# Second block's experts: a fixed order on the tensor engine, and the first overflow block as a seventeenth expert

## The chip, the cores and the metric

The kernel runs on one core of a Trainium2 chip. The core has a tensor engine (PE, with its weight loads shown apart as PEld), a vector engine (DVE), a scalar engine (ACT), GpSimd (POOL) and a sync engine (SP) that here issues the weight transfers. Each engine has its own instruction stream and waits for the others on semaphores. The metric is the device time of one execution in microseconds. Before the change it was 1744.35 us, the median of 3 runs (1742.81 to 1746.68).

## The reference, cut to what matters

Two transformer trunks run one after the other on 256 tokens of width 1024, in float32. The change touches only the last stage: the mixture of experts of the second trunk. Each token picks 2 of 16 experts; an expert is a gated network with weights `w1`, `w3` (1024 x 512) and `w2` (512 x 1024). A final norm follows.

```python
def moe(x, router_w, router_b, w1, w3, w2):
    ...
    gates = jnp.sum(jax.nn.one_hot(eidx, N_EXPERTS, dtype=F32_2) * w[..., None], axis=1).astype(x.dtype)
    out = jnp.zeros_like(x)
    for e in range(N_EXPERTS):
        h = jax.nn.silu(x @ w1[e]) * (x @ w3[e])
        out = out + gates[:, e:e + 1] * (h @ w2[e])
    return out
...
        y = moe(hl2.reshape(B * S, D), router_w, router_b, lp['moe_w1'], lp['moe_w3'], lp['moe_w2'])
        xl = xl + g2_l * y.reshape(B, S, D)
...
    return rmsnorm(xl, final_g)
```

## The kernel before, in words

All weights of the program come through one ring of seven buffers of 2 MB (`RING = 7`), filled by transfers that SP issues in one fixed order (`Stream`, L317). A buffer is given to the next transfer when its last reader is done. In the last stage each expert has three such transfers, `w1`, `w3` and `w2`, so 48 for the 16 experts.

Experts are not run on all 256 tokens. After the router, `rank` holds each token's place in the list of its expert, and a block of 64 places per expert is computed. Where an expert has more than 64 tokens, the rest forms overflow blocks of 64 more places; up to seven such blocks are listed (`ji` holds their experts, `n_jobs` their number), and they are run after the sixteen experts in nested branches on `n_jobs` (L1872 to L1877).

Two experts with even and odd number form a pair and share their tiles:

- `take` (L1764) builds a one-hot matrix `oh` of the places on DVE, multiplies the normed tokens `n` by it (16 matmuls, L1777, with the two experts' 64 places side by side), and scales and shifts the result into `xg` in turns on DVE and ACT (L1784, L1781). Then it builds a second one-hot matrix `ohg` that holds the gates (L1788), transposes it on PE (L1792) and copies it to `sT` on ACT.
- `mlp` (L1796) is a generator with four steps per expert. Step 1: 16 matmuls with `w1` (L1807) and silu on ACT (L1814, `sg`). Step 2: 16 matmuls with `w3` and the product `hid` on DVE (L1818). Step 3: two transposes of `hid` on PE (L1822) and a copy to `hidT` on ACT (L1824). Step 4: 8 matmuls with `w2` (L1832) and the multiplication with the trunk's gate row into `Y` on DVE (L1837).
- `scatter` (L1751) multiplies `sT` with the `Y` of both experts (4 matmuls, L1755), and adds the result to `x` on DVE (L1756).

A matmul on float32 stands as two instructions in the profile and as one in the built program.

The loop (L1909 to L1920) writes the steps of expert e and expert e-1 alternately, and adds the scatter of an earlier pair and the `take` of the next one after odd experts. The order in which PE runs them is not the written one: the framework's scheduler sorts the instructions of each engine by its own estimate of when each is ready.

An overflow block (`job`, L1847) reads its expert number into an SP register, issues three transfers, selects its places (L1863 to L1867), and does `take`, the four steps and `scatter` with nothing else between. After it come the sums of squares on ACT, the products with the final norm's row on DVE and POOL (L1928), the root, and the output.

Of the kernel before, what the change touches and what calls it, by code (L numbers as in the profile page):

```python
# [19 lines left out]
D = 1024  # L20
S = 256
# [335 lines left out]
def trunk_kernel(ctx: ExitStack, tc: tile.TileContext, I: dict, O: dict):  # L357
# [1321 lines left out]
    def moe2(ss):  # L1679
        shsc = ada[2, 1]  # L1680
        with tc.tile_pool(name="moe2", bufs=1, reuse_waits="tile") as wk:
# [76 lines left out]
            def tiles(t="", nb=2):  # L1758
                k = dict(bufs=nb)
                return dict(oh=wk.tile([128, 2, 128], F32, name="oh" + t, **k), og=wk.tile([128, 2, 128], F32, name="ohg" + t, **k),  # L1760
                            xg=wk.tile([128, 8, 128], F32, name="xg" + t, **k), sT=wk.tile([128, S], F32, name="sT" + t, **k),
                            Y=wk.tile([128, D], F32, name="Y" + t, **k))

            def take(cols_, t, w=64):  # L1764

                m = w * len(cols_)
                oh, og, xg, sT = t["oh"], t["og"], t["xg"], t["sT"]
# [4 lines left out]
                for d4 in range(2):  # L1772
                    p = bank()
                    for j in range(4):
                        dt = 4 * d4 + j
                        for b in range(2):
                            T.matmul(p[:, j * 128:j * 128 + m], n[:, b, dt * 128:(dt + 1) * 128], oh[:, b, :m], start=b == 0, stop=b == 1)  # L1777
                    for j in range(4):
# [4 lines left out]
                        else:  # L1783
                            V.tensor_scalar(xg[:, dt, :m], p[:, j * 128:j * 128 + m], shsc[:, 1, dt:dt + 1],  # L1784
                                            shsc[:, 0, dt:dt + 1], op0=OP.mult, op1=OP.add)
                for b in range(2):
                    for i, (sl, gt) in enumerate(cols_):
                        v = V.tensor_scalar(og[:, b, w * i:w * i + w], it, sl[:, b:b + 1], gt[:, b:b + 1],  # L1788
                                            op0=OP.is_equal, op1=OP.mult)
                p = bank()  # L1790
                for b in range(2):
                    T.transpose(p[:m, b * 128:(b + 1) * 128], og[:, b, :m], ident)  # L1792
                A.copy(sT[:m], p[:m, :256])
                return v

            def mlp(e, xg, i, Y, get=None):  # L1796

                c = slice(64 * i, 64 * i + 64)
# [3 lines left out]
                def up(nm):  # L1802
                    w = weights(nm)
                    p = bank("u", 3)
                    for kt in range(8):
                        for h in range(2):
                            T.matmul(p[rows[h], :256], xg[:, kt, c], w[kt // 4][:, kt % 4, h * 256:(h + 1) * 256], start=kt == 0, stop=kt == 7)  # L1807
                    if get is None:
                        free((nm, e), 2)
                    return p  # L1810

                pg = up("w1")
# [3 lines left out]
                pu = up("w3")  # L1816
                hid = wk.tile([128, 256], F32, name="hid", bufs=2)
                V.tensor_tensor(hid, pu[:, :256], sg, op=OP.mult)  # L1818
                yield
# [208 lines left out]
```

## Time and profile before

| what | value |
| --- | --- |
| median of 3 runs | 1744.35 us (1742.81 to 1746.68) |
| profiled execution, own time | 1742.27 us |
| its span, first to last instruction | 1740.5 us |
| PE busy / PEld busy | 1313.8 us (75%) / 723.0 us (42%) |
| DVE busy / ACT busy / POOL busy | 487.8 us (28%) / 249.4 us (14%) / 10.7 us (1%) |
| data moved | 636.01 MB, mean 365 GB/s |
| mean granted clock of PE | 0.896 |

All rows below are of the profiled execution, whose own time is 1742.27 us: 1740.5 us of span and 1.77 us around it. The last stage begins at about 1432 us with the second trunk's second norm and runs to the end. Durations are of one instruction or of a merged run of equal instructions. A run of matmuls is shown with the time to the end of the last; the next run can start before that, so what a group costs PE is read from one start to the next. Bracketed numbers are idle time of the engine just ahead of the row, and what ended it.

### The profile page before, as it was taken

The numbers are of one execution on the slowest core, as the hardware profiler recorded it, in microseconds if no ns is written. First come the engines' busy times: TensorE is split into PE (matmuls) and PEld (weight loads), VectorE is DVE, ScalarE is ACT, GpSimd is POOL, SyncE is SP. The second block draws the span as 40 slices with busy tenths as digits, with TensorE's granted clock in tenths as the row PEclk, the third lists the DMA queues.
The fourth block names the chain that finished last, engine by engine and source line by source line (L and its number), as shares of the span: only waits on it lengthen the run. The fifth ranks groups of instructions, "written<-read, shape, count | busy, mean of one in ns | idle before, by whom it ended". The sixth has DMA issues, their size and how long they took to land. (4 is left out here: it accounts for less than half of the span.)

```text
span 1740.5 us, 24033 instructions
## 1 busy us (share of the span) xinstructions
PE 1313.8 (75%) x10612; PEld 723.0 (42%) x10612; DVE 487.8 (28%) x1051; ACT 249.4 (14%) x567; POOL 10.7 (1%) x19
## 2 busy tenths in 40 slices
PE   5997757756565569988575665657799998999996
PEld 2444423323222234545232232224487656555453
DVE  2444212402010029441111020100245726233223
ACT  3021100100000022511100000000223422111012
POOL 0000000000000000000000000000000000000000
PEclk9998988978888879998888787889999998999998
DMA  9978899999999998469999999999942765999970
GB/s 378 413 314 365 363 428 428 427 427 427 428 427 428 427 415 340 160 271 427 428 427 427 427 427 427 428 427 428 427 158 90 297 249 221 427 427 427 421 310 26
DMA packets 46972, 636.01 MB, mean 365 GB/s; under 512 B 6192, under 2 KB 6320, under 8 KB 8464
## 3 DMA queue, kind: packets, MB, share of 16 engines
q1 hardware_dynamic: 44624, 630.82, 86.6%
q0 software_dynamic: 1952, 3.09, 0.6%
q8 instruction: 85, 1.39, 0.3%
q10 hardware_dynamic: 288, 0.52, 0.1%
q14 instruction: 23, 0.19, 0.0%
HBM read 633.42 MB, written 1.05 MB: 365 GB/s over the span
## 5 line engine op out<-in xcount | busy, mean ns | idle before, releaser
L1065 PE MATMUL b<-w,xg 128*32 128x256 f32 x4096 | 316.6, 465 | 219.4 <-DMA w<-in_moe_w_up_dram 134.6
L1065 PEld LDWEIGHTS b<-w,xg 128*32 128x32 f32 x4096 | 148.9, 129 | 385.0 <-issue 137.7
L1065 PE MATMUL b<-w,hidT 128*32 128x256 f32 x2048 | 160.7, 467 | 83.2 <-DMA w<-in_moe_w_down_dram 77.7
L1085 DVE TENSOR_TENSOR hid<-b,sg 128x256 f32<-128x256 f32 x32 | 13.6, 425 | 504.0 <-PE b L1065 410.9
L1065 PEld LDWEIGHTS b<-w,hidT 128*32 128x32 f32 x2048 | 76.4, 129 | 154.5 <-DMA w<-in_moe_w_down_dram 62.3
L1807 PE MATMUL u<-w,xg 128*64 128x256 f32 x1088 | 125.0, 384 | 0.0
L1093 DVE SCALAR_TENSOR_TENSOR Y<-b,cc,gq 32x256 f32<-32x256 f32 x128 | 61.5, 480 | 211.7 <-PE b L1065 210.1
L499 DVE SCALAR_TENSOR_TENSOR w<-w,cond 128x1024 f32<-128x1024 f32 x77 | 97.0, 1280 | 4.9 <-DMA w<-in_ada21s_dram 3.2
L1807 PEld LDWEIGHTS u<-w,xg 128*64 128x64 f32 x1088 | 78.3, 138 | 47.5 <-issue 11.7
L1080 ACT ACTIVATE sg<-b 128x256 f32<-128x256 f32 x32 | 12.3, 383 | 416.4 <-PE b L1065 416.3
L1832 PE MATMUL b<-w,hidT 128*64 128x512 f32 x272 | 63.2, 598 | 9.8 <-ACT hidT L1824 9.8
L1090 ACT COPY hidT<-b 128x256 f32<-128x256 f32 x32 | 11.9, 372 | 320.6 <-PE b L1088 320.6
L707 PE MATMUL b<-w,n 128*128 128x512 f32 x128 | 56.0, 594 | 0.0
L1837 DVE TENSOR_TENSOR Y<-b,hkb 64x512 f32<-64x512 f32 x34 | 23.4, 688 | 72.2 <-PE b L1832 71.9
L1191 PE MATMUL b<-w,hT 128*128 128x512 f32 x96 | 43.4, 608 | 0.0
L832 PE MATMUL b<-w,hT 128*128 128x512 f32 x96 | 41.6, 593 | 1.7 <-DMA w<-in_fc_dram 1.7
L1777 PE MATMUL b<-oh,n 128*128 128x128 f32 (+1 forms) x288 | 39.3, 297 | 3.2 <-DVE oh L1771 3.2
L1777 PEld LDWEIGHTS b<-oh,n 128*128 128x128 f32 x288 | 36.8, 209 | 9.2 <-issue 6.3
L1106 PE MATMUL b<-Y,gT 128*128 128x512 f32 x64 | 32.6, 646 | 9.7 <-DVE Y L1093 9.7
L1000 PE MATMUL b<-oh,n 128*128 128x128 f32 x256 | 35.6, 305 | 0.9 <-DVE oh L1045 0.9
L1832 PEld LDWEIGHTS b<-w,hidT 128*64 128x64 f32 x272 | 18.6, 136 | 42.2 <-issue 28.3
L707 PEld LDWEIGHTS b<-w,n 128*128 128x128 f32 x128 | 24.0, 190 | 28.8 <-issue 28.7
(444 smaller groups left out, 1345.2 us busy)
## 6 DMA issues: line engine op xcount, KB each, us to landing
w<-in_moe_w_gate_dram SPq DMA_DIRECT2D x64, 2048.0 KB, 30.8
w<-in_moe_w_up_dram SPq DMA_DIRECT2D x64, 2048.0 KB, 30.9
w<-in_moe_w_down_dram SPq DMA_DIRECT2D x64, 2048.0 KB, 30.9
w<-in_moe_w_dram SPq DMA_DIRECT2D x51, 2048.0 KB, 14.9
w<-in_wi_dram SPq DMA_DIRECT2D x5, 2048.0 KB, 22.4
w<-in_ada00s_dram SPq DMA_DIRECT2D x4, 2048.0 KB, 22.6
w<-in_ada01s_dram SPq DMA_DIRECT2D x4, 2048.0 KB, 25.5
w<-in_ada10s_dram SPq DMA_DIRECT2D x4, 2048.0 KB, 11.5
```

Of the source, the lines that this page charges most:

```text
L499: V.scalar_tensor_tensor(into[:, hs], w[:, hs], c, into[:, hs], op0=OP.mult, op1=OP.add)
L707: T.matmul(acc, mixT[:, kt, b * 128:(b + 1) * 128], w(kt)[:, h * 512:(h + 1) * 512], start=kt == first, stop=kt == last)
L832: T.matmul(p, hT[:, kt, b * 128:(b + 1) * 128], w(kt), start=kt == 0, stop=kt == 7)
L1000: T.matmul(p[:, j * 128:(j + 1) * 128], n[:, b, dt * 128:(dt + 1) * 128], oh[:, b, g * 128:(g + 1) * 128], start=b == 0, stop=b == 1)
L1065: T.matmul(p[32 * q:32 * q + 32, :256], lhs(kt), w[:, k, q * 256:(q + 1) * 256], start=kt == 0, stop=kt == 7)
L1093: V.scalar_tensor_tensor(Y[32 * j:32 * j + 32, q * 256:(q + 1) * 256], pd[32 * q:32 * q + 32, :256], cc[32 * q:32 * q + 32, e:e + 1], gq[3 ...
L1106: T.matmul(p, gT[:, b * 128:(b + 1) * 128], Y[:, h * 512:(h + 1) * 512], start=True, stop=True)
L1191: T.matmul(p, hT[:, kt, b * 128:(b + 1) * 128], w(kt), start=kt == 0, stop=kt == 7)
L1777: T.matmul(p[:, j * 128:j * 128 + m], n[:, b, dt * 128:(dt + 1) * 128], oh[:, b, :m], start=b == 0, stop=b == 1)
L1807: T.matmul(p[rows[h], :256], xg[:, kt, c], w[kt // 4][:, kt % 4, h * 256:(h + 1) * 256], start=kt == 0, stop=kt == 7)
L1832: T.matmul(pd[rows[h]], hidT[:, kt % 2, rows[kt // 2]], w[kt // 2][:, kt % 2, h * 512:(h + 1) * 512], start=kt == 0, stop=kt == 3)
L1837: V.tensor_tensor(Y[c, h * 512:(h + 1) * 512], pd[rows[h]], gq2[rows[h]], op=OP.mult)
```

## The change: what it does

1. `take` is cut into `take` (gathering) and `way_back` (gates, transposes, copy to `sT`), and each step of `mlp`, as well as `take`, `scatter` and `way_back`, returns its last PE instruction. `turn_of` runs a step with every PE instruction ordered behind the last one of the step before (`tc.issue_after`). So PE runs the loop in the written order, and the scheduler has no choice there. The order on the other engines is not tied.
2. In the loop the `take` of the next pair, the scatter of the earlier pair and `way_back` now come after the even expert of a pair instead of the odd one.
3. The first overflow block is no longer inside a branch: its places are selected ahead of the loop (`job_slots(0)`), its weights are requested when expert 14 is written, and it runs as expert number 16 in the loop, with tiles of its own for `sT` and `Y` (`sTz`, `Yz`), whether or not an overflow exists.
4. Its scatter comes last, after the branches for the other six possible blocks.

```diff
             def scatter(sT, Y, k):
...
-                        T.matmul(p, sT[:k, b * 128:(b + 1) * 128], Y[:k, h * 512:(h + 1) * 512], start=True, stop=True)
+                        last = T.matmul(p, sT[:k, b * 128:(b + 1) * 128], Y[:k, h * 512:(h + 1) * 512], start=True, stop=True)
...
+                return last
...
+            tail = []
+
+            @contextmanager
+            def in_turn():
+                with ExitStack() as held:
+                    if tail:
+                        held.enter_context(tc.issue_after(tail[-1].ins))
+                    yield
...
-            def mlp(e, xg, i, Y, get=None):
+            def mlp(e, t, i, get=None):
...
-                if e in (E - 1, None):
+                if e is None:
                     table_of_roots(hidT[0:1, 0, 0:1])
-                yield
+                yield last
...
-            def jobs(j=0):
+            def jobs(j=1):
...
+            def turn_of(f):
+                with in_turn():
+                    last = f()
+                if last is not None:
+                    tail.append(last)
...
+            first_job = job_slots(0)
             for e in range(E + 1):
-                cur = mlp(e, ts[e // 2]["xg"], e % 2, ts[e // 2]["Y"]) if e < E else iter(())
-                next(cur, 0)
-                next(prev, 0)
-                next(cur, 0)
-                next(prev, 0)
-                if e % 2 == 1 and e >= 3:
-                    t = ts.pop((e - 3) // 2)
-                    scatter(t["sT"], t["Y"], 128)
-                if e % 2 == 1 and e + 1 < E:
-                    ts[(e + 1) // 2] = pair(e + 1)
+                cur = mlp(e, ts[e // 2], e % 2) if e < E else mlp(None, ts[E // 2], 0, first_ws)
+                for g in (cur, prev, cur, prev):
+                    turn_of(lambda: next(g, None))
+                if e % 2 == 0 and e < E:
+                    t2 = ts[e // 2 + 1] = dict(own="" if e + 2 < E else "z")
+                    cs = both_of(e + 2) if e + 2 < E else first_job
+                    turn_of(lambda: take(cs, t2))
+                    if e:
+                        t = ts.pop(e // 2 - 1)
+                        turn_of(lambda: scatter(t["sT"], t["Y"], 128))
+                    turn_of(lambda: way_back(cs, t2))
+                    if e + 2 == E:
+                        first_ws = job_weights(0)
                 prev = cur
+            turn_of(lambda: next(prev))
             t = ts.pop(E // 2 - 1)
-            scatter(t["sT"], t["Y"], 128)
+            turn_of(lambda: scatter(t["sT"], t["Y"], 128))
+            turn_of(lambda: next(prev))
             jobs()
+            t = ts.pop(E // 2)
+            scatter(t["sT"], t["Y"], 64)
```

How the instructions stand on PE. First one pair in the middle of the loop, before the change, from one scatter to the next. L1755 is the scatter, L1807 the matmuls with `w1` or `w3`, L1777 the `take`, L1792 the transposes to `sT`, L1822 those of `hid`, L1832 the matmuls with `w2`:

```order
L1755 MATMUL b<-Y,sT 128x512 x4
L1807 MATMUL u<-w,xg 64x256 x16
L1777 MATMUL b<-oh,n 128x128 x9
L1807 MATMUL u<-w,xg 64x256 x16
L1777 MATMUL b<-oh,n 128x128 x7
L1792 MATMUL b<-cst,ohg 128x128 x2
L1822 MATMUL b<-cst,hid 128x128 x2
L1832 MATMUL b<-w,hidT 64x512 x8
L1807 MATMUL u<-w,xg 64x256 x32
L1822 MATMUL b<-cst,hid 128x128 x2
L1832 MATMUL b<-w,hidT 64x512 x8
```

The same pair after the change, on PE (L1765 is the scatter now, L1825 the matmuls with `w1` or `w3`, L1787 the `take`, L1810 and L1840 the transposes, L1850 those with `w2`):

```order
L1787 MATMUL b<-oh,n 128x128 x16
L1765 MATMUL b<-Y,sT 128x512 x4
L1810 MATMUL b<-cst,ohg 128x128 x2
L1825 MATMUL u<-w,xg 64x256 x16
L1840 MATMUL b<-cst,hid 128x128 x2
L1825 MATMUL u<-w,xg 64x256 x16
L1850 MATMUL b<-w,hidT 64x512 x8
L1825 MATMUL u<-w,xg 64x256 x16
L1840 MATMUL b<-cst,hid 128x128 x2
L1825 MATMUL u<-w,xg 64x256 x16
L1850 MATMUL b<-w,hidT 64x512 x8
```

The same matmuls stand there. Before, the two transposes of `hid` stood directly in front of the matmuls with `w2` of the same expert; now 16 matmuls with the next expert's `w3` stand between them, and the `take` is in one piece.

The end of the loop on PE before, from the last expert to the overflow block's `take` (L1777 with 64 columns) and on to its scatter:

```order
L1807 MATMUL u<-w,xg 64x256 x32
L1822 MATMUL b<-cst,hid 128x128 x2
L1832 MATMUL b<-w,hidT 64x512 x8
L1755 MATMUL b<-Y,sT 128x512 x4
L1906 TENSOR_LOAD jobi
L1875 COMPARE_AND_BRANCH
L1777 MATMUL b<-oh,n 128x64 x16
L1792 MATMUL b<-cst,ohg 64x128 x2
L1807 MATMUL u<-w,xg 64x256 x32
L1822 MATMUL b<-cst,hid 128x128 x2
L1832 MATMUL b<-w,hidT 64x512 x8
L1755 MATMUL b<-Y,sT 128x512 x4
```

And now on PE, from the overflow block's `w1` (its `take` stands further up, among expert 14 and 15) to the branch:

```order
L1825 MATMUL u<-w,xg 64x256 x16
L1840 MATMUL b<-cst,hid 128x128 x2
L1825 MATMUL u<-w,xg 64x256 x16
L1850 MATMUL b<-w,hidT 64x512 x8
L1840 MATMUL b<-cst,hid 128x128 x2
L1765 MATMUL b<-Y,sT 128x512 x4
L1850 MATMUL b<-w,hidT 64x512 x8
L1935 TENSOR_LOAD jobi
L1904 COMPARE_AND_BRANCH
```

The overflow block's steps moved in between those of expert 15, and the scatter of the last pair moved ahead of the block's `w2`. PE's last rows now, after the six branch bodies, are these:

```order
L1825 MATMUL u<-w,xg 64x256 x32
L1840 MATMUL b<-cst,hid 128x128 x2
L1850 MATMUL b<-w,hidT 64x512 x8
L1765 MATMUL b<-Y,sT 128x512 x4
L1904 UNCONDITIONAL_BRANCH x7
L1765 MATMUL b<-Yz,sTz 128x512 x4
```

The last row is new there: before, PE had no matmul behind the branches.

## Rows read from the trace of the kernel before

**Rows 1.** Stretches: us, busy (count) of PE, PEld, DVE, ACT, POOL; clock, DMA share, GB/s
```profile
1520.00:1560.00 40.00, 38.03 (x242) 20.02 (x240) 13.40 (x28) 3.50 (x9) 0.00 (x0) 1.00 1.01 427
1703.00:1714.00 11.00, 8.93 (x51) 7.30 (x52) 3.75 (x15) 2.94 (x6) 0.00 (x0) 0.69 0.01 1
```

**Rows 2.** Waits of PE from 1447 us to the end: total us, times, longest
```profile
PE b L1832 <- ACT hidT L1824: 9.8, 15, 0.9
PE b L1822 <- DVE hid L1818: 4.7, 8, 0.6
```

**Rows 3.** Timeline of PE, one pair: start, us, engine, line, operation, count, idle before
```profile
1542.98 7.08 PE L1807 MATMUL u<-w,xg 128*64 128x256 f32 x64
1550.64 0.44 PE L1822 MATMUL b<-cst,hid 128*128 128x128 f32 x2 [0.58 <-DVE hid L1818]
1551.59 3.65 PE L1832 MATMUL b<-w,hidT 128*64 128x512 f32 x16 [0.52 <-ACT hidT L1824]
1555.18 3.70 PE L1755 MATMUL b<-Y,sT 128*128 128x512 f32 x8
1558.81 3.67 PE L1807 MATMUL u<-w,xg 128*64 128x256 f32 x32
...
1571.35 3.65 PE L1832 MATMUL b<-w,hidT 128*64 128x512 f32 x16 [0.86 <-ACT hidT L1824]
1574.84 7.08 PE L1807 MATMUL u<-w,xg 128*64 128x256 f32 x64
```

**Rows 4.** Timeline of PE near the loop's start
```profile
1471.80 3.84 PE L1777 MATMUL b<-oh,n 128*128 128x128 f32 x32
...
1475.79 3.67 PE L1807 MATMUL u<-w,xg 128*64 128x256 f32 x32
1479.39 0.44 PE L1822 MATMUL b<-cst,hid 128*128 128x128 f32 x2
1479.76 3.67 PE L1807 MATMUL u<-w,xg 128*64 128x256 f32 x32
1483.26 3.60 PE L1832 MATMUL b<-w,hidT 128*64 128x512 f32 x16
1486.80 0.44 PE L1822 MATMUL b<-cst,hid 128*128 128x128 f32 x2
```

**Rows 5.** SP's weight transfers from 1456 us on: count, issue times, time to landing
```profile
L317 SPq DMA_DIRECT2D w<-in_moe_w_dram x43: 327/328/383, 1456.5 to 1663.9; - x43
...
L1855 SPq DMA_DIRECT2D w<-in_moe_w_dram x3: 332/343/353, 1670.6 to 1677.5; - x3
...
DMA to landing us min/median/max: 7.8/15.2/23.5
```

**Rows 6.** Timeline of DVE: the last part of the second pair's one-hot matrix
```profile
1462.00 0.25 DVE L1771 TENSOR_SCALAR oh<-cst,rank 128x64 f32<-128x64 f32 x1
```

**Rows 7.** Timeline of PE, last expert and overflow block
```profile
1694.89 3.65 PE L1832 MATMUL b<-w,hidT 128*64 128x512 f32 x16 [0.52 <-ACT hidT L1824]
1699.34 3.70 PE L1755 MATMUL b<-Y,sT 128*128 128x512 f32 x8 [0.79 <-DVE Y L1837]
1705.11 5.57 PE L1777 MATMUL b<-oh,n 128*128 128x64 f32 x32 [2.07 <-DVE oh L1771]
...
1720.92 3.65 PE L1832 MATMUL b<-w,hidT 128*64 128x512 f32 x16 [0.46 <-ACT hidT L1824]
1725.36 3.70 PE L1755 MATMUL b<-Y,sT 64*128 64x512 f32 x8 [0.79 <-DVE Y L1837]
```

**Rows 8.** Timeline of DVE from the overflow block's `Y` on
```profile
1724.62 1.41 DVE L1837 TENSOR_TENSOR Y<-b,hkb 64x512 f32<-64x512 f32 x2 [4.66 <-PE b L1832]
...
1730.22 3.23 DVE L1928 TENSOR_TENSOR n<-x,fg 128x512 f32<-128x512 f32 x2 [0.44 <-PEq L1875]
```

**Rows 9.** Line 1875: PE's branches, ns min/median/max, first and last start
```profile
L1875 PEldq COMPARE_BRANCH  x3: 92/193/3674, 1700.7 to 1730.0; - x3
```

More of the change, by code (lines that the diff above doesn't have):

```diff
@@ L1 @@
 import math
-from contextlib import ExitStack
+from contextlib import ExitStack, contextmanager
 import numpy as np
@@ L1776, in take @@
                         for b in range(2):
-                            T.matmul(p[:, j * 128:j * 128 + m], n[:, b, dt * 128:(dt + 1) * 128], oh[:, b, :m], start=b == 0, stop=b == 1)
+                            last = T.matmul(p[:, j * 128:j * 128 + m], n[:, b, dt * 128:(dt + 1) * 128], oh[:, b, :m], start=b == 0, stop=b == 1)
                     for j in range(4):
@@ L1831, in mlp @@
                     for h in range(2):
-                        T.matmul(pd[rows[h]], hidT[:, kt % 2, rows[kt // 2]], w[kt // 2][:, kt % 2, h * 512:(h + 1) * 512], start=kt == 0, stop=kt == 3)
+                        last = T.matmul(pd[rows[h]], hidT[:, kt % 2, rows[kt // 2]], w[kt // 2][:, kt % 2, h * 512:(h + 1) * 512], start=kt == 0, stop=kt == 3)
                 if get is None:
@@ L1835, in mlp @@
                 gq2 = gqs[2, 1]
+                if "Y" not in t:
+                    t["Y"] = place("Y", [128, D], t)
                 for h in range(2):
-                    V.tensor_tensor(Y[c, h * 512:(h + 1) * 512], pd[rows[h]], gq2[rows[h]], op=OP.mult)
-                yield
+                    V.tensor_tensor(t["Y"][c, h * 512:(h + 1) * 512], pd[rows[h]], gq2[rows[h]], op=OP.mult)
+                yield last
             keys = wk.tile([128, 3, 16], F32, name="keys")
@@ L1858, in job @@
                 ws = {nm: load(nm) for nm in ("w1", "w3", "w2")}
[L1859 to L1869 removed]
+                return lambda nm: ws[nm]
+            def job(j):
+                ws, t = job_weights(j), {}
+                cs = job_slots(j)
+                take(cs, t)
+                way_back(cs, t)
+                run(mlp(None, t, 0, ws))
                 scatter(t["sT"], t["Y"], 64)
[L1872 removed]
+            def jobs(j=1):
                 if j == JOBS:
@@ L1877, in jobs, with both_of @@
                     jobs(j + 1)
-            def pair(e0):
-                t = tiles()
-                t["last"] = take([(rank[:, :, e], gates[:, :, e]) for e in (e0, e0 + 1)], t)
-                return t
+            def both_of(e0):
+                return [(rank[:, :, e], gates[:, :, e]) for e in (e0, e0 + 1)]
             banks.close()
             pair_ps.append(ctx.enter_context(tc.tile_pool(name="ps2", bufs=5, space=PSUM)))
-            ts = {0: pair(0)}
+            ts = {0: {}}
+            take(both_of(0), ts[0])
+            way_back(both_of(0), ts[0])
             queue_behind.append(ts[0]["last"])
```

62 lines of the change are left out of this document (33 added, 29 removed).

## Prediction, made before the changed kernel was run

> **What bounds the kernel now.** The page's chain of waits only covers the last microseconds, the output, so I read the last stage by other views. First the stretches [rows 1]: in the middle of the expert loop PE is busy 38.03 of 40 us at full granted clock, and the DMA engines are busy all the time at 427 GB/s. Two resources are near their limit together, so the question is which one leaves slack. PE's list of waits [rows 2] answers it: from 1447 us to the end PE waits for no weight at all, only for its helpers, 9.8 us for `hidT` (15 times) and 4.7 us for `hid` (8 times). PE sets the pace. Its timeline of one pair [rows 3] shows 31.86 us from one double `w1`/`w3` run to the next (1542.98 to 1574.84), and in it the three waits of a pair: 0.58, 0.52 and 0.86 us, 1.96 in all. They stand where transposes of `hid` or matmuls with `w2` directly follow what they need. At the end [rows 7] the same waits stand in the open: from the last expert's `w2` (1694.89) to the overflow block's `w2` (1720.92) PE goes through two more waits, an idle stretch of 2.07 us for the new `oh`, and a stretch at 0.69 of the clock [rows 1], in which the block's `take` lasts 5.57 us. Three transfers on line 1855 [rows 5] show that this input has one overflow block, so that running it always adds no work.
>
> **The fixed order.** No matmul is added or removed; what matters is how long each step lasts when nothing is waited for. Near the loop's start PE once runs them so, at full clock, and I take start to start [rows 4]: `take` with the transposes for `sT` 3.99 us (1471.80 to 1475.79), 16 matmuls with `w1` 3.60, transposes of `hid` 0.37, `w3` 3.50, `w2` 3.54. A scatter takes 3.63 (1555.18 to 1558.81) [rows 3]. One expert is 3.60 + 0.37 + 3.50 + 3.54 = 11.01 us, and a pair 2 x 11.01 + 3.99 + 3.63 = 29.64 us. Against 31.86 that is 2.2 us less, the three waits and a little more. The waits go because 3.50 us of `w3` now lie between a transpose and its `w2`, where the ACT copy had cost up to 0.86, and because `hid` has a whole step of time. What the scatter needs, `Y`, takes DVE 1.41 us [rows 8] and lies beside the `take`. The `take`'s results go to `xg` on DVE and ACT while PE scatters, and are first read by PE 15 us later (a scatter, the transposes, one expert). I cost these at nothing; if an evacuation is late by a PSUM bank, PE stands behind it with all that is queued, at most the length of one such wait, 0.9 us [rows 2], per pair.
>
> **The weights.** Six transfers of 2048 KB at 427 GB/s [rows 1] take 6 x 4.91 = 29.5 us per pair, just under PE's 29.64, so the second limit stays 0.1 us away. Most transfers are issued when a buffer comes free; by the ring's rule (first released, first filled) `w1` of expert e+2 gets the buffer of `w1` of expert e, and so on. The tightest is used 29.64 - 3.60 = 26.0 us after its issue, and no transfer took more than 23.5 us to land [rows 5]. A lead is there too: the transfers run from 1456.5 us; the eighth from there, `w1` of expert 4, lands at about 1456.5 + 2.9 + 8 x 4.91 = 1498.7 (the 2.9 from issue to start is an estimate, the shortest landing of 7.8 us less one transfer), and PE wants it at 1507.4 by the sum below. Cost taken: 0. Bound: with no backlog, the three transfers issued 3.6, 7.5 and 11.0 us into a pair end at 3.6 + 2.9 + 14.7 = 21.2, and the next, issued at 22.2, starts at 25.1, so DMA would be dry for 3.9 us; after that its queue never empties.
>
> **The opening.** The second pair's `take` now stands ahead of expert 1. It needs the one-hot matrix whose last part DVE ended at 1462.25 [rows 6]; a few small DVE steps of the overflow block's selection come in between, so 1462.8. Then 3.99 us: 1466.8, expert 1 until 1477.8. PE idles about 1.6 us here that it did not before.
>
> **The loop and the end.** Seven pairs, experts 2 to 15, with the block's `take` costed like the others (its loads have the same 128 columns): 1477.8 + 7 x 29.64 = 1685.3. Then the block's `w1`, expert 15's transposes and the block's `w3`: 7.47, 1692.8. Expert 15's `w2` starts there; its scatter starts 4.45 later, as in [rows 7] (1694.89 to 1699.34), since `Y` is still waited for: 1697.2; with 3.63, the block's `w2` starts at 1700.8, instead of 1720.92: **20.1 us earlier**.
>
> **Behind the branch.** The last scatter stood 4.44 us behind the block's `w2`, half a `Y` in (1720.92 to 1725.36). Now branches lie between; each engine reports there that it is done, so the scatter waits for both halves of `Y`: 3.70 + 1.41 + about 0.2 = 5.3, **0.9 later**. The branch itself must be counted on PE, since matmuls follow it now. PE's longest branch lasted 3.67 us [rows 9]. PE's sequencer reaches it while the block's `w2` is queued, and 5.3 us hide it: 0. Were it to begin only when `w2` has ended, the scatter starts at 3.65 + 3.67 = 7.3, 2.0 later: the other bound. The Trainium skill (Runtime: NRT & Kernel Launch, Instruction fetch mechanics) says that a taken branch to code outside the fetched window stalls until that code is fetched, which speaks against a branch in this place; the trace has the 3.67 us that would be such a stall, though not what caused it. By that rule with nothing hiding it the end is 2.0 us later.
>
> **The final norm.** Before, a branch's end at 1729.8 stood between the last addition to `x` and all that follows; the two products on DVE then took 3.23 us beside POOL [rows 8]. Now squares and products of the first quarters can run between the four additions. That can give up to 2.7 us (only one product left behind the last addition), or nothing, if POOL beside the additions stretches them as it stretched the products (1.6 us each, against 0.7 for other DVE operations of that size). I take 1.5 less.
>
> **Sum.** -20.1 + 0.9 - 1.5 = -20.7 us. From the profiled execution's 1742.27 us: **1721.6 us**. The runs' median lies 2.1 us above that execution, which I leave in the range.
>
> **Rivals.**
> - The waits come back elsewhere. PE can no longer pass a step that is not ready, and each pair has a `take`, scatter and transposes in one place, whose PSUM banks (five) DVE and ACT must empty in time. With 1.96 us per pair back in seven pairs: 13.7 more, 1735. For it: DVE and ACT take turns on `xg`. Against: DVE is busy 13.4 of 40 us [rows 1].
> - Weights bound. DMA has 0.1 us per pair to spare. If it runs dry as above: 1725.5. Against: the lead of about 9 us, and that a dry spell makes the next burst queue.
> - Slower: PE's granted clock. It was 1.0 (2.4 GHz) through the loop in spite of gaps of up to 0.86 us, but after the gap of 2.07 the stretch shows 0.69 [rows 1, 7], that is, part of it at 1.2 GHz. If the fixed order makes one gap of about 2 us per pair, each costs what that one did, about 2 us for the gap and 3.4 (31% of 11 us): 5.4 x 7 = 38, 1759. From four such gaps on nothing is left of the gain. Against: no step in the new order needs what was made just before, but at the end. The Trainium skill (TensorE: Matmul & The Clock Gate, HAM oscillation) describes loops in which each waiting gap lowers the clock again; by it the gap is the thing to look for, and the trace agrees for the one of 2.07 us only.
> - The change doesn't do what it says: the scheduler lets other PE work in, or the block's transfers are late. Then the end alone is won: 26.0 us from expert 15's `w2` to the block's before, now 8.0 and the 3.99 + 7.47 us of the block's steps that moved into the loop, so 6.5, and with - 0.9 + 1.5 some 7.1 us: 1735.
>
> **Chances.** Forecast 0.79, waits back 0.10, weights 0.06, clock 0.03; not as it says 0.02. The forecast's own range is 1717 to 1727: final norm, branch and the 2 us between executions. With half of the first rival the range becomes **1715 to 1732**. 0.2% (3.5 us) is what a measurement can tell from no change: faster 0.94, same 0.02, slower 0.04.
>
> **What will show it.** In the loop a pair should take 29.6 us on PE, with no wait for `hid` or `hidT` inside. The opening should show one wait for `oh`. The block's `w2` should start near 1701, DMA stay above 420 GB/s until about 1685, the clock at 1.0 until the last scatter, and the squares begin between the additions. A pair of 31 us or more, waits of PE on weights, or a last scatter over 6 us behind the block's `w2` would make it wrong.

## The result, and the profile after

The changed kernel takes 1717.39 us, the median of 4 runs (1716.69 to 1719.27), against 1743.58 us (1741.39 to 1746.68, 4 runs) before: a ratio of 0.985 with a 95% interval of 0.9833 to 0.9868. The profiled execution's own time is 1719.27 us, its span 1717.5 us; that is 23.0 us less than the profiled execution before. The medians lie 26.2 us apart, since the profiled execution is here the slowest of its kernel and was before below its median. The forecast was 1721.6 us, 1715 to 1732.

The stretch in the loop first, then two around the last scatter, to be laid beside [rows 1] (columns as there):

```profile
1520.00:1560.00 40.00, 40.00 (x281) 23.14 (x281) 14.39 (x37) 6.12 (x15) 0.00 (x0) 1.00 1.01 428
1697.00:1703.00 6.00, 4.36 (x19) 1.45 (x19) 2.10 (x4) 0.00 (x0) 0.00 (x0) 1.00 0.03 7
1703.00:1710.00 7.00, 5.80 (x8) 1.76 (x6) 3.88 (x6) 2.55 (x7) 2.52 (x2) 0.51 0.00 0
```

PE is now busy for all 40 us of the loop's stretch, where it was for 38.03, and the DMA engines still move 428 GB/s. The last row holds what was not foreseen: PE's clock is at its lower level, 1.2 GHz, through nearly all of the last scatter. PE's waits from 1447 us to the end, all of them, in place of [rows 2]:

```profile
PE b L1787 <- DVE oh L1781: 1.8, 2, 1.1
PE b L1765 <- DVEq L1904: 1.6, 1, 1.6
PE b L1765 <- DVE Y L1857: 0.4, 1, 0.4
```

No wait for `hid` or `hidT` is left, and none for weights. One pair on PE, from `take` to `take`, in place of [rows 3] (L1787 `take`, L1765 scatter, L1810 transposes to `sT`, L1825 `w1` and `w3`, L1840 transposes of `hid`, L1850 `w2`):

```profile
1546.15 3.84 PE L1787 MATMUL b<-oh,n 128*128 128x128 f32 x32
1549.82 3.60 PE L1765 MATMUL b<-Y,sT 128*128 128x512 f32 x8
1553.26 0.38 PE L1810 MATMUL b<-cst,ohg 128*128 128x128 f32 x2
1553.57 3.67 PE L1825 MATMUL u<-w,xg 128*64 128x256 f32 x32
1557.17 0.44 PE L1840 MATMUL b<-cst,hid 128*128 128x128 f32 x2
1557.54 3.67 PE L1825 MATMUL u<-w,xg 128*64 128x256 f32 x32
1561.05 3.60 PE L1850 MATMUL b<-w,hidT 128*64 128x512 f32 x16
1564.48 3.62 PE L1825 MATMUL u<-w,xg 128*64 128x256 f32 x32
...
1575.44 0.82 PE L1787 MATMUL b<-oh,n 128*128 128x128 f32 x5
```

There is no bracket in it, so nothing is waited for, and the pair takes 1575.44 - 1546.15 = 29.29 us. The opening and the end on PE, in place of [rows 4, 7]:

```profile
1460.74 0.71 PE L1787 MATMUL b<-oh,n 128*128 128x128 f32 x4
1462.15 3.39 PE L1787 MATMUL b<-oh,n 128*128 128x128 f32 x28 [0.70 <-DVE oh L1781]
...
1465.69 3.67 PE L1825 MATMUL u<-w,xg 128*64 128x256 f32 x32
...
1476.60 3.62 PE L1825 MATMUL u<-w,xg 128*64 128x256 f32 x32
...
1681.65 3.62 PE L1825 MATMUL u<-w,xg 128*64 128x256 f32 x32
...
1689.08 3.60 PE L1850 MATMUL b<-w,hidT 128*64 128x512 f32 x16
1692.61 0.44 PE L1840 MATMUL b<-cst,hid 128*128 128x128 f32 x2
1693.47 3.70 PE L1765 MATMUL b<-Y,sT 128*128 128x512 f32 x8 [0.42 <-DVE Y L1857]
1697.10 3.65 PE L1850 MATMUL b<-w,hidT 128*64 128x512 f32 x16
1702.40 6.40 PE L1765 MATMUL b<-Yz,sTz 64*128 64x512 f32 x8 [1.64 <-DVEq L1904]
```

The block's `w2` starts at 1697.10 instead of 1720.92, and the last scatter 5.30 us behind it. That scatter lasts 6.40 us where it lasted 3.70. The weight transfers, in place of [rows 5]:

```profile
L317 SPq DMA_DIRECT2D w<-in_moe_w_dram x43: 327/328/383, 1456.3 to 1652.6; - x43
...
DMA to landing us min/median/max: 7.8/19.3/23.9
```

The median landing rose from 15.2 to 19.3 us, and the longest is 23.9. The branch itself, line 1904 (ns min/median/max, start), in place of [rows 9]:

```profile
L1904 PEldq COMPARE_BRANCH  x1: 3762/3762/3762, 1697.7 to 1697.7; - x1
...
L1904 DVEq EVENT_SEMAPHORE  x1: 21/21/21, 1702.2 to 1702.2; - x1
```

PE's branch lasts 3.76 us, from 1697.7 to 1701.5, beside the block's `w2` and the wait for `Yz`; what ends the scatter's wait is DVE's report at 1702.2, when both halves of `Yz` are done.

### The profile page after: what moved, and what is told of

It reads as the page before. It is cut to its first block, busy times and chain, and to the rows that moved or that the text cites. A ratio compares the mean times of both kernels' runs of the same rounds, so it can differ in the third digit from the quotient of the medians.

```text
span 1717.5 us, 24011 instructions
## 1 busy us (share of the span) xinstructions
PE 1312.8 (76%) x10612; PEld 721.0 (42%) x10612; DVE 484.9 (28%) x1051; ACT 248.1 (14%) x564; POOL 10.3 (1%) x19
## 3 DMA queue, kind: packets, MB, share of 16 engines
q0 software_dynamic: 1952, 3.09, 0.6%
## 5 line engine op out<-in xcount | busy, mean ns | idle before, releaser
L1825 PE MATMUL u<-w,xg 128*64 128x256 f32 x1088 | 124.3, 381 | 0.0
L1825 PEld LDWEIGHTS u<-w,xg 128*64 128x64 f32 x1088 | 75.9, 137 | 43.3 <-issue 8.6
L1850 PE MATMUL b<-w,hidT 128*64 128x512 f32 x272 | 61.3, 592 | 0.0
L1787 PEld LDWEIGHTS b<-oh,n 128*128 128x128 f32 x288 | 34.7, 200 | 8.6 <-issue 6.9
L1787 PE MATMUL b<-oh,n 128*128 128x128 f32 (+1 forms) x288 | 36.5, 287 | 1.8 <-DVE oh L1781 1.8
L1000 PEld LDWEIGHTS b<-oh,n 128*128 128x128 f32 x256 | 34.7, 222 | 4.3 <-issue 2.9
L1836 DVE TENSOR_TENSOR hid<-u,sg 128x256 f32<-128x256 f32 x17 | 7.2, 424 | 100.2 <-issue 74.5
```

What stands on the lines that cost most here:

```text
L1000: T.matmul(p[:, j * 128:(j + 1) * 128], n[:, b, dt * 128:(dt + 1) * 128], oh[:, b, g * 128:(g + 1) * 128], start=b == 0, stop=b == 1)
L1787: last = T.matmul(p[:, j * 128:j * 128 + m], n[:, b, dt * 128:(dt + 1) * 128], oh[:, b, :m], start=b == 0, stop=b == 1)
L1825: last = T.matmul(p[rows[h], :256], xg[:, kt, c], w[kt // 4][:, kt % 4, h * 256:(h + 1) * 256], start=kt == 0, stop=kt == 7)
L1850: last = T.matmul(pd[rows[h]], hidT[:, kt % 2, rows[kt // 2]], w[kt // 2][:, kt % 2, h * 512:(h + 1) * 512], start=kt == 0, stop=kt == 3)
```

## The experiments

Executions reach the last stage at times up to 8 us apart, so positions are counted from the start of expert 0's `w1`, at which the clock has just reached its full level (1452.78 us before, 1452.58 after). The expectations of e3, e5, e8 and e9 count from the first matmul of line 1736, which lies 8.9 to 10.0 us ahead of that (9.13 in the changed kernel), with the clock's rise in between; so compare differences between kernels. "Scatter" is the last one, `r` the root's first step on DVE (L652), "end" the end of the span.

| kernel | expert 2's `w1` | block's `w2` | scatter, its length | `r` | end |
| --- | --- | --- | --- | --- | --- |
| before | 23.00 | 268.14 | 272.58, 3.70 | 280.60 | 287.72 |
| changed | 24.02 | 244.52 | 249.81, 6.40 | 257.79 | 264.92 |
| changed, again (a2) | 24.07 | 244.57 | 249.87, 3.67 | 256.27 | 263.40 |
| loop alone (e1) | 24.07 | 250.01 | 254.45, 3.70 | 262.47 | 269.58 |
| order free (e2) | 23.58 | 259.08 | 264.38, 6.28 | 272.23 | 279.36 |
| transposes at `w2` (e11) | 24.60 | 253.85 | 259.14, 5.69 | 266.40 | 273.54 |
| old places (e4) | 23.05 | 245.03 | 250.32, 3.67 | 256.71 | 263.85 |
| scatter, then branch (e3) | 24.07 | 244.57 | 249.01, 3.70 | 257.51 | 264.63 |
| no branch (e5) | 24.02 | 244.52 | 248.96, 4.68 | 255.38 | 262.52 |
| pair's scatter behind `w2` (e6) | 24.07 | 241.04 | 249.75, 3.67 | 256.15 | 263.28 |
| both of these (e7) | 24.02 | 240.99 | 248.20, 3.70 | 254.63 | 261.75 |
| opening (e8) | 23.01 | 243.56 | 248.85, 5.43 | 255.86 | 262.99 |
| opening, use order (e9) | 23.05 | 243.61 | 248.90, 5.75 | 256.23 | 263.36 |
| candidate (e12) | 23.06 | 240.08 | 248.78, 5.45 | 255.80 | 263.28 |

The times tell e1, e2 and e11 from the changed kernel. Those of e3, e4, e5, e6, e8, e9 and e12 have ratios of 0.984 to 0.986, like the changed kernel's, with intervals that overlap; what is said of them rests on positions in one trace each.

### Which part paid

**e1: the loop alone.**

```diff
-            for e in range(E + 1):
+            for e in range(E):
...
-            jobs()
-            t = ts.pop(E // 2)
-            scatter(t["sT"], t["Y"], 64)
+            jobs(0)
```

> Parts 1 and 2 of the change alone: PE's order is fixed, and the overflow block stays in its branch after the experts, as before. Theory (the sum is made of separate terms): the loop's share stays whole. After the change expert 14's `w2` started at 1678.22 and the step behind it at 1681.65; here expert 15 comes without the block's `take` and its two transposes (3.9 us), so its transposes stand at about 1677.8, its `w2` at 1678.6 after a wait of 0.5 for `hidT`, the scatter 4.45 later at 1683.1. Before, the same scatter started at 1699.34, so 16.2 us are won and the span is about 1740.5 - 16.2 = 1724.3, some 6.8 us above the changed kernel's 1717.5. Pair 29.3 us. Rival (the gain needs both parts, because the block's steps in the loop are what covers expert 15's waits): under 10 us won, span above 1730. Clock rival: the gap of about 2 us ahead of the block's `take` is back, with a stretch at the lower clock level, but that was there before too, so it changes neither figure.

Measured: 1724.5 us, ratio 0.9902 (0.9879 to 0.9926), span 1722.7. The block's `w2` is 18.1 us earlier than before the change; the theory holds, the rival's 10 us do not. The gap ahead of the block's `take` is back, and its row answers to one of [rows 7]:

```profile
1690.57 3.79 PE L1787 MATMUL b<-oh,n 128*128 128x64 f32 x32 [2.07 <-DVE oh L1781]
```

The same gap of 2.07 us, the same matmuls: 3.79 us here, 5.57 before. So the stretch at the lower clock, which the expectation had counted in as fixed, does not belong to that gap; from the last pair's scatter to the end of the span it is 37.9 us where 41.2 were taken over from before. Against that stand 1.2 us by which that scatter came later than summed, counted from expert 0's `w1`: with no `take` in front, the scatter after expert 14 waits 0.8 us for `Y`. Together, and with a start 0.5 us later, the span came out 1.6 us below the 1724.3 expected.

**e2: parts 3 and 4 with the order left free.**

```diff
             def turn_of(f):
-                with in_turn():
-                    last = f()
-                if last is not None:
-                    tail.append(last)
+                f()
```

> Parts 3 and 4 alone, with the new written order but no instruction tied to another: the scheduler may sort PE's work again. As built, transposes of `hid` stand directly in front of `w2` again in five of the seven pairs after the opening, as before the change. Theory (what the order won is the waits for `hid` and `hidT`): those pairs cost about 2 us more (three waits, 1.96 us per pair before the change), pair about 31.3 us, 10 to 12 us in all, span about 1728 to 1730, and PE waits for `hid` and `hidT` again. Rival (the writing order alone does it, the tie is idle): span within 3 us of 1717.5 and no such waits.

Measured: 1734.23 us, ratio 0.995 (0.9934 to 0.9967). PE's waits:

```profile
PE b L1850 <- ACT hidT L1842: 6.7, 13, 0.5
PE b L1840 <- DVE hid L1836: 4.5, 8, 0.6
```

They sum to 11.2 us, as expected, but the block's `w2` is 14.6 us later than in the changed kernel. Part of the other 3 us shows in a pair's timeline on PE, where the scheduler cuts `take` and scatter in two:

```profile
1574.60 3.17 PE L1787 MATMUL b<-oh,n 128*128 128x128 f32 x26
1577.69 3.67 PE L1825 MATMUL u<-w,xg 128*64 128x256 f32 x32
1581.30 0.94 PE L1787 MATMUL b<-oh,n 128*128 128x128 f32 x6
1582.07 2.74 PE L1765 MATMUL b<-Y,sT 128*128 128x512 f32 x6
1584.74 3.67 PE L1825 MATMUL u<-w,xg 128*64 128x256 f32 x32
1588.35 1.13 PE L1765 MATMUL b<-Y,sT 128*128 128x512 f32 x2
1589.31 0.38 PE L1810 MATMUL b<-cst,ohg 128*128 128x128 f32 x2
```

From start to start the `take` costs 3.09 + 0.77 = 3.86 us instead of 3.67, the scatter 2.67 + 0.96 = 3.63 instead of 3.44: 0.4 us per pair in the four pairs that are cut like this, about half of the 3 us; where the rest goes is open. The written order alone does not hold; the tie holds it.

**e11: fixed, but the transposes in front of their `w2`.**

```diff
-                for g in (cur, prev, cur, prev):
+                for g in (cur, cur, prev, prev):
```

> The change with one thing undone inside its fixed order: a step's transposes of `hid` stand directly in front of the same expert's `w2` again (`w1` e, `w3` e, transposes e-1, `w2` e-1) instead of one 3.5 us step ahead of it. Times from the start of expert 0's `w1`, from where the clock is at its full level. Theory (a fixed order is worth what stands between a helper's result and its use): `w2` waits for ACT's copy to `hidT`, 0.52 us each time as at the end of the kernel before, 16 times: 8.3 us, pair 30.3 instead of 29.29, block's `w2` at 244.5 + 8.3 = 252.8. Rival (the forecast's first rival at full size, waits of 1.96 us per pair whatever is written): block's `w2` near 258. Rival (the tie alone is what helps, the place of the transposes does nothing): 244.5 and no wait for `hidT`.

Measured: 1729.11 us, ratio 0.9912 (0.9892 to 0.9932). One line of waits holds it:

```profile
PE b L1850 <- ACT hidT L1842: 8.2, 16, 0.5
```

The block's `w2` comes at 253.85, 9.3 us late: the sixteen waits of 0.52 us, and some 1 us that is in no wait. So these 9.3 us of the 14.6 that the free order loses hang on the 3.5 us of `w3` between the transposes and their `w2`. The other 5.2 (259.08 to 253.85) the tie gives without that distance: `hid` still has a whole `w1` and `w3` of time here, and PE never waits for it, where e2 waited 4.5 us.

**e4: fixed, with `take` and scatter behind the odd expert, where they were.**

```diff
-                if e % 2 == 0 and e < E:
+                if e % 2 == 1 and e >= 3:
+                    t = ts.pop((e - 3) // 2)
+                    turn_of(lambda: scatter(t["sT"], t["Y"], 128))
+                if e % 2 == 1:
...
```

> Part 1, 3 and 4 with part 2 undone: PE's order is fixed, but `take`, scatter and transposes to `sT` stand after the odd expert, as they were written before (scatter first, then `take`, then the transposes, then the next pair's `w1`). On DVE the one-hot matrix `ohg` comes behind the last of `xg`, so the transposes wait: from the end of the `take` 2.1 us to the last `xg` (1549.82 to 1551.90 after the change) and 1.0 us for `ohg`, about 3 us per pair on PE, and nothing can pass. Theory A (the forecast's slow rival: a gap of about 2 to 3 us per pair also lowers the granted clock): 3.0 + 3.4 us per pair, 7 pairs 45 us, less 1.8 us for the opening's wait that goes: span about 1760, and the clock at its lower level for a part of every pair. Theory B (a gap costs only itself): 21 - 1.8 us, span about 1736, clock 1.0 through the loop. Theory C (place does not matter once the order is fixed): span about 1716.

Measured: 1719.11 us, ratio 0.986 (0.9844 to 0.9877). Theories A and B fall at their premise: `ohg` is made a pair ahead (DVE wrote the next one at 1565.46, after the transposes of 1563.95), so they never waited, and no gap came into the pairs; the clock rival was not put to the test. C is nearest: a pair from `take` to `take` lasts 29.29 us here too (1560.38 to 1589.67). But it is not all of it: expert 2 is 1.0 us earlier than in the changed kernel, and the block's `w2` 0.5 us later. Most of these 1.5 us is a wait that the changed kernel does not have:

```profile
PE u L1825 <- DMA w<-in_moe_w_dram: 1.1, 2, 0.8
```

### The end

**a2: the changed kernel once more.**

> The changed kernel once more, unaltered, for a second trace and for times on the same chip as the version above. Theory (all differences from one profiled execution to the next lie in when the stage is reached and when the clock falls): from the start of expert 0's `w1` the block's `w2` at 244.5 and the last scatter at 249.8 again, within 0.1 us; the last scatter lasts 3.7 to 6.4 us, by the moment of the clock's fall alone. Rival (the fall of the clock 0.8 us into the last scatter belongs to this kernel): 6.40 us again.

Measured: 1719.07 us, ratio 0.9857 (0.984 to 0.9875). All positions up to the last scatter agree within 0.06 us, and then:

```profile
1704.81 3.67 PE L1765 MATMUL b<-Yz,sTz 64*128 64x512 f32 x8 [1.64 <-DVEq L1904]
```

The same instructions behind the same gap of 1.64 us last 3.67 us, at full clock. So 6.40 us was one execution's, and the end is 1.5 us earlier without it. The clock falls in a2 as well, but only at about 1712 us, when PE is done (columns as in [rows 1]):

```profile
1704.81:1708.48 3.67, 3.67 (x8) 1.39 (x8) 2.16 (x4) 1.48 (x5) 1.76 (x2) 1.00 0.01 2
1713.00:1716.00 3.00, 0.00 (x0) 0.00 (x0) 0.59 (x2) 1.14 (x2) 0.00 (x0) 0.50 0.64 242
```

**e3: part 4 undone, the scatter ahead of the branches.**

```diff
-            jobs()
             t = ts.pop(E // 2)
             scatter(t["sT"], t["Y"], 64)
+            jobs()
```

> Part 4 of the change undone: the block's scatter stands ahead of the six branches, as before. All times from the start of the first matmul of line 1736, since executions reach this stage at times up to 2.4 us apart. In the changed kernel the last scatter starts at 258.95 and the root's first step `r` (line 652) at 266.93 where the clock was low in that scatter, and 6.40 us behind the scatter's start where it was not. Theory (the branches cost about what the norm wins): the scatter starts half a `Y` earlier, at 253.65 + 4.44 = 258.1, and `r` about 8.0 us behind it, as before the change (1725.36 to 1733.38): 266.1, that is 0.8 us later than 258.95 + 6.40 = 265.3, and DVE's products and the squares start only behind the branch. Rival (part 4 was worth the 2.7 us by which the norm was measured shorter): 268 or later. Rival (part 4 loses, by the branch on PE's way): `r` below 264.5.

Measured: 1719.52 us, ratio 0.9856 (0.9839 to 0.9872). The scatter starts at 249.01, 0.86 earlier than in a2, and `r` comes at 257.51, 1.24 later: part 4 wins 2.10 us behind the scatter and pays 0.86 for it. The theory is nearest; it had 8.0 us from the scatter to `r`, and 8.50 were measured. On DVE:

```profile
1710.09 3.43 DVE L1974 TENSOR_TENSOR n<-x,fg 128x512 f32<-128x512 f32 x2 [0.73 <-DVEq L1904]
1713.45 0.15 DVE L652 TENSOR_TENSOR r<-ss 128x2 f32<-128x2 f32 x1
```

As in [rows 8], both products stand behind the branch and stretch to 3.43 us.

**e5: no branches** (further overflow blocks are left out).

```diff
-            jobs()
             t = ts.pop(E // 2)
```

> The six branches for further overflow blocks are left out altogether (this input has none to run). Theory (what the branch costs here is the half of `Y` that the scatter waits longer, 0.9 us, and nothing of the 3.76 us that PE's branch lasts): the block's scatter starts 4.44 instead of 5.30 us behind its `w2`, at 258.1 from line 1736's first matmul; at full clock `r` follows 6.4 us later, at 264.5. Rival (the branch's 3.76 us are on the path in part): the scatter starts more than 1.5 us earlier than the 258.95 of the changed kernel. On the clock: of the gaps seen, 2.07 us lowered it before the change and not in the run with the loop alone, 1.64 us lowered it after the change and not in the run with the old places; so a gap of 0.8 us may or may not, and no figure is set on it.

Measured: 1716.44 us, ratio 0.9841 (0.9824 to 0.9857).

```profile
1695.52 3.65 PE L1850 MATMUL b<-w,hidT 128*64 128x512 f32 x16
1699.96 4.68 PE L1765 MATMUL b<-Yz,sTz 64*128 64x512 f32 x8 [0.79 <-DVE Yz L1857]
```

4.44 us from `w2` to scatter, as the theory has it: the branch costs 0.85 us, the wait for the second half of `Yz`, and PE's 3.76 us are hidden.

**e6 and e7: the last pair's scatter behind the block's `w2`**, with the branches (e6) and without them (e7; further overflow blocks are left out).

```diff
             t = ts.pop(E // 2 - 1)
-            turn_of(lambda: scatter(t["sT"], t["Y"], 128))
             turn_of(lambda: next(prev))
+            turn_of(lambda: scatter(t["sT"], t["Y"], 128))
```

> The whole change, but the last pair's scatter stands behind the block's `w2` instead of ahead of it: PE has 3.5 us of work while DVE makes `Yz` and the branches are taken. The block's `w2` starts at about 1693.5 (after a wait of 0.5 for `hidT`), the scatter at 1697.1, and DVE ends its four additions at about 1701.5; then the last scatter starts at about 1701.6 instead of 1702.40, after a gap of about 0.8 us on PE instead of 1.64. Theory (the gap of 1.64 us is what lowered the clock in the last scatter, 6.40 us instead of 3.70): it lasts 3.7 us, together 0.8 + 2.7 = 3.5 us less than the profiled 1717.5, span about 1714. Rival (the clock falls there whatever the gap): 0.8 us less, span about 1716.7, last scatter above 6 us. Rival (the branches set its start): last scatter at 1702.4 or later.

> No branches (the further overflow blocks are left out) and the last pair's scatter behind the block's `w2`: PE has no gap at all ahead of the last scatter. Times from the start of expert 0's `w1`. The block's `w2` starts at 241.0, the pair's scatter at 244.6, the block's scatter at 248.1 at once. Theory (the clock falls inside the last scatter because of a gap ahead of it; with gaps of 0.8 to 1.64 us it did in five of seven traces): no gap, so the last scatter lasts 3.7 us at full clock. Rival (the fall comes from something else): it lasts over 4.5 us here too. With the clock full, `r` follows the scatter's start by 6.4 us, at 254.5.

Measured: e6 1719.22 us, ratio 0.9859 (0.9839 to 0.9878); e7 1711.55 us in one run. Of the 7.7 us by which e7 is shorter than the changed kernel's profiled execution, 4.6 lie ahead of expert 0's `w1` (1448.03 against 1452.58) and are not the edit's. The last scatter of e6 starts only 0.1 us earlier, so of its start the last rival holds, since DVE now reaches the branch behind its four additions (the last ends at 1703.85) and reports 0.6 us after that; line 1904 in e6:

```profile
L1904 PEldq COMPARE_BRANCH  x1: 3422/3422/3422, 1697.4 to 1697.4; - x1
...
L1904 DVEq COMPARE_BRANCH  x1: 72/72/72, 1703.8 to 1703.8; - x1
...
L1904 DVEq EVENT_SEMAPHORE  x1: 21/21/21, 1704.4 to 1704.4; - x1
```

e7 has no gap and the scatter lasts 3.70 us, as its theory has it; but e6 has a gap of 1.42 us and lasts 3.67, so the gap's length does not decide. In eleven traces with a gap of 0.79 us or more ahead of a last scatter behind the moved block, seven show the clock falling in it (4.68 to 6.40 us) and four do not (3.67 to 3.70), with either result at 0.79, at 1.41 to 1.42 and at 1.64 us. In those four, and in e7, the clock falls only after the scatter's end, as in a2. What decides its moment in one execution stays open; the expectation's "five of seven" was five of eight at that point.

### The opening

**e8: the second pair's `take` behind expert 1's `w1`; e9: and the weights in the order of use.**

```diff
-                for g in (cur, prev, cur, prev):
+                for i, g in enumerate((cur, prev, cur, prev)):
+                    turn_of(lambda: next(g, None))
+                    if e == 1 and i == 0:
+                        turn_of(lambda: take(cs, t2))
+                if e == 1:
+                    turn_of(lambda: way_back(cs, t2))
...
```

```diff
-    for e in range(E):
-        for nm in ("w1", "w3", "w2"):
+    for e in range(E + 1):
+        for nm, k in (("w1", e), ("w3", e), ("w2", e - 1)):
...
```

> The change, with the second pair's `take` behind expert 1's `w1` and its transposes behind expert 0's `w2`, so that PE has no wait for `oh` at the opening (0.70 us, and about 1.1 more by order): expert 2's `w1` starts about 1.8 us earlier than the changed kernel's 33.15 us after line 1736's first matmul. Theory (weights: six transfers take 6 x 4.91 = 29.47 us per pair and PE's pair 29.29, so the lead is being used up, and the run with the old places, 1.07 us ahead at the opening, lost 0.85 and 0.20 us to `w3` loads near 1639 and 1668): what is won at the opening is given back in waits of PE for weights, 1 to 1.8 us in all, and the last scatter starts at 258.3 to 259.3 instead of 258.95. Rival (the waits in that run came from its own order of use): no wait for weights, the last scatter at 257.2.

> The same with one more edit: the weight transfers are issued in the order in which PE now uses them (`w1` and `w3` of expert e, then `w2` of expert e-1), no longer by expert. The matmuls are the same and so is PE's order. Theory (the transfers are short of lead only for `w1` and `w3`, because each `w2` is brought 11 us before its use, one place too early): each `w1` and `w3` gains about one transfer, 4.9 us, of lead, PE waits for no weight, and the opening's 1.8 us stay won: last scatter at 257.2, 1.8 us before the changed kernel's 258.95, span from line 1736 about 271 to 272. Rival (DMA's total bounds the stage, whatever the order): waits of 1 us and more for weights as in the kernel without this edit, last scatter at 258.3 or later. Rival (the other order takes buffers out of turn at the start): PE waits for weights in the first two pairs.

Measured: e8 1717.55 us, ratio 0.9851 (0.9835 to 0.9868); e9 1718.78 us, ratio 0.9854 (0.9837 to 0.987). The opening gives 1.0 us, not 1.8, and the whole of it arrives at the last scatter (248.85 against 249.81). Neither has a wait for weights, so the theory on e8 falls: being 1 us ahead does not exhaust the lead, and e9 had nothing to win. The rival on e8, that the waits of e4 came from its own order, is what is left. In e4 the odd expert is not behind a `take`, a scatter and two transposes, so it needs its weights 3.67 + 3.44 + 0.31 = 7.4 us earlier in the pair, and the two loads that were late are `w3` of experts 13 and 15. That this is the reason is argued from the order, not tried by itself.

**e12: e6 and e8 with all products of the norm on POOL.**

```diff
-                    (V if b else G).tensor_tensor(n[:, b, hs], x[:, b, hs], fg[:, hs], op=OP.mult)
+                    G.tensor_tensor(n[:, b, hs], x[:, b, hs], fg[:, hs], op=OP.mult)
```

> A complete version with three edits to the change: the second pair's `take` behind expert 1's `w1` (1.0 us won at expert 2's `w1` in the run that moved the opening alone), the last pair's scatter behind the block's `w2`, and all four products with the final norm's row on POOL, so that none stands between DVE's last additions (in the run with the scatter moved, a product of 1.38 us kept the fourth addition waiting from 1708.2 to 1709.42). Times from the start of expert 0's `w1`. Theory: the last scatter starts at 249.75 - 0.96 = 248.8; at full clock `r` comes 5.3 instead of 6.40 us later, at 254.1, and POOL's fourth product ends 1.91 + 4 x 1.25 = 6.9 us behind the scatter's start, just when the root is there: end about 261.4, 3.5 us before the changed kernel's profiled 264.92, of which 2.7 is clock. Rival (POOL's products slow DVE's small steps or come too late): `r` to end longer than 7.12 us by over 1 us, nothing won over the 262.99 of the run with the opening alone.

Measured: 1717.88 us, ratio 0.986 (0.984 to 0.988), beside 0.9857 for a2 on the same chip: nothing won that can be measured. The scatter starts 1.1 us earlier than in a2, as summed, but the clock fell in it, and the end is 7.48 us behind the start of `r` instead of 7.13; the 0.35 us are `r` itself, which POOL held up (last section).

## Why the prediction was right, and where its sizes were off

**The fixed order.** Right, and by its reason: no wait inside a pair, and e11 brings back 0.52 us per expert when the `w3` between is taken away. Its size was off: 29.29 us per pair, not 29.64, in seven pairs 2.4 us. I had added start-to-start times taken ahead of other neighbours. A scatter costs 3.63 us ahead of a `w1` [rows 3] but 3.44 ahead of the transposes to `sT` (1549.82 to 1553.26); `w2` 3.54 ahead of transposes [rows 4] but 3.43 ahead of a `w1` (1561.05 to 1564.48). `take` with its transposes was right: 3.67 + 0.31 against 3.99.

**The opening.** Expert 2's `w1` came at 1476.60, not 1477.8. I let the `take` begin when the whole one-hot matrix was there; its first four instructions ran ahead on the first part, and PE waited 0.70 us, not 1.6. With these two terms and 0.1 in the end's steps (15.45 us from the block's `w1` to its `w2`, summed 15.55) the block's `w2` is 23.8 us earlier instead of 20.1 (from the span's start; 23.6 from expert 0's `w1`).

**The weights.** Cost 0 was right, but not by the 0.1 us per pair that were to be left: a pair of 29.29 us is shorter than the 29.5 us that its six transfers take by the sum. What is left to cover it is the lead named beside it: the longest landing was 23.9 us, where the tightest use comes, by the prediction's sum with the pair as measured, 29.29 - 3.60 = 25.7 us after its issue, and PE waited for no weight, not even in e8, where it is 1 us earlier. DMA moved 426 to 435 GB/s up to 1670 us and 394 from there to 1685, where it was to stay above 420; the loop ended 3.7 us sooner than summed. That the weights are close shows in e4, whose order had 1.1 us of waits for them.

**The branch.** Right: 5.30 us from `w2` to scatter, forecast 5.3; e5 shows 4.44 without it. PE's branch lasts 3.38 to 3.90 us in the nine traces that have it ahead of the last scatter, and in all nine it is DVE's report that ends the scatter's wait, so nothing of it is paid. The Trainium skill (Runtime: NRT & Kernel Launch, Instruction fetch mechanics) says that a taken branch to code outside the fetched window stalls until that code is fetched. No run here shows whether these microseconds are such a stall.

**The final norm.** Forecast 1.5 us less; from the scatter's start to `r` it is 8.02 us before and 6.40 in a2: 1.6 less. In the profiled execution the low clock in the scatter took it all back (7.98): PE's results then come 1.71 us apart, and DVE follows them. I had expected full clock until the last scatter and named no price for its fall there.

**The sum.** From expert 0's `w1` to the end: -23.6 (block's `w2`) + 0.85 (behind the branch) - 0.04 (norm, at low clock) = -22.8 us, where -20.7 was forecast; in a2 it is -24.3. That the profiled execution comes so near is in part luck: 3.5 us more at the block's `w2` and 1.5 less in the norm, by the clock, partly cancel.

**The rivals.** Waits that come back and late weights did not occur. The parts can be set beside each other now. At the block's `w2` the order alone wins 18.1 us (e1) and the block in the loop 9.1 (e2, the case "not as it says", forecast 1735, measured 1734.23), both together 23.6. Both traces also lack the low clock that the execution before had behind its gap of 2.07 us, e2 without the gap, but e1 with it, so that in e1 it is no gain of the order: from that `take` to the block's `w2` it is 15.81 us before (1705.11 to 1720.92) and 12.55 in e1 (1690.57 to 1703.12), 3.3 less. Counted once, that gives 14.9 + 5.8 + 3.3 = 24.0 against 23.6, so the two parts add up within 0.4 us, and 3.3 of the 23.6 are a comparison with one execution at a low clock. The clock rival's price was wrong: it took 3.4 us per gap from one sample, and in e1 the same gap of 2.07 us cost nothing in clock. The forecast names that stretch, but its 20.1 us hold these 3.3 us without setting them apart. No kernel here had a gap of about 2 us in every pair, so what many such gaps would do was not tried; sixteen of about 0.5 us in e11 left the clock at 1.00 (1465 to 1700 us).

## What to carry to other kernels

Where one engine is busy nearly all the time and its waits are for short helper steps, put one other step of its own between handing work to the helper and using the result, and tie the order: here the tie without the distance gives 9.3 us away, and an untied order 14.6. When steps are summed from a trace, take each start-to-start time in front of the neighbour that it will have. A clock change seen once behind a gap is a sample and not a price: run the kernel before it again, or compare it with a second trace, before it goes into a sum.

## What the hardware showed that was not expected

A DVE product of two tensors waits while POOL multiplies. In a2 it takes twice its 0.69 us, and holds the fourth addition behind it:

```profile
1708.39 1.38 DVE L1974 TENSOR_TENSOR n<-x,fg 128x512 f32<-128x512 f32 x1
1709.69 0.68 DVE L1766 TENSOR_TENSOR x<-x,b 128x512 f32<-128x512 f32 x1
1710.40 0.69 DVE L1974 TENSOR_TENSOR n<-x,fg 128x512 f32<-128x512 f32 x1
```

POOL's products in a2 run from 1706.72 to 1709.21; the first DVE product ends 0.56 us later, the second, with POOL done, takes 0.69. In e12 `r`, a step of 0.16 us, lasted 0.51 us and ended with POOL's product (1707.78 + 1.26 = 1709.04):

```profile
1708.55 0.51 DVE L652 TENSOR_TENSOR r<-ss 128x2 f32<-128x2 f32 x1 [0.85 <-ACT b L623]
```

The additions, which read one operand from PSUM, kept their 0.69 us beside POOL. The Trainium skill (SBUF — State Buffer, Who interferes with whom) has this as a rule: a DVE instruction with two inputs in SBUF contends with a GpSimd instruction that reads SBUF, and outside certain modes one with at most one such input does not. The traces agree, by these rows.

The clock fell within the last scatter in one execution of the changed kernel and after it in another, at the same gap. The Trainium skill (TensorE: Matmul & The Clock Gate, What's actually happening) says that the gate's watch on the engine runs freely and does not start anew with a kernel, so that the same kernel has more or fewer slow matmuls from run to run. It says so of the clock's rise at a kernel's start; here the fall varies in the same way, with 3.67 us in a2 against 6.40 in the first profile.
